# Where the feed-forward weights lie in memory against the activations: 192 bytes off modulo 512 for six products of seven, and one tile for both halves of a weight

## The chip, the core and the metric

The kernel runs on one core of one Trainium2 chip. The metric is the device time of one execution in microseconds (us); before the change it is 2301.29 us, the median of three runs (2299.22, 2301.29 and 2302.05). A core has a matrix engine (PE, TensorE), a vector engine (DVE), a scalar engine (ACT), a small-core engine (POOL) that does next to nothing here, and a queue processor (SP) that issues every DMA of this kernel. Operands of a matmul are read from SBUF, where each of 128 partitions has its own byte addresses; results go to PSUM.

## What is computed

One layer of a hybrid encoder over 512 tokens of width 2048: a normalised input projection, two groups of mixer heads (a gated recurrence called HGRN2, and stick-breaking attention), an output projection with a residual, and then a SwiGLU feed-forward part. The change is about this last part, with a hidden width of 5632 = 44 x 128:

```python
h = rms_norm(x, norm2_g[layer]) * (1.0 + sc2) + sh2
gate, up = jnp.split(h @ w_ffn_in[layer], 2, axis=-1)
x = x + g2 * ((jax.nn.silu(gate) * up) @ w_ffn_out[layer])
```

## The kernel before, in words

**Precision.** TensorE multiplies in the type float32r. To keep float32 accuracy, every operand is split in two halves, a rounded "high" half and the remainder, the "low" half, and each product becomes three matmuls: high x high, high x low, low x high (function `product`, L908; `three`, L227). The function `split` (L212) makes the halves of a weight: ACT casts the raw tile to the high half (L220), DVE subtracts it from the raw tile to give the low half (L221).

**The first feed-forward product** (`h @ w_ffn_in`) is the loop at L1115 over f = 2 to 43, one slice of 128 gate columns and 128 up columns each (f = 0 and 1 are done earlier in another form). Instead of eight block products each f needs seven, by Winograd's scheme: DVE forms sums of weight blocks (L1122 to L1125), and PE runs the products in the order 1, 2, 6, 7, 5, 4, 3. A product is 8 steps of three matmuls, 24 in all, with a stationary weight block of 128x128 and a moving block of activations of 128x256. The activations lie in four tiles, opA (products 1 and 2), opB (6 and 7), opC (5 and 4) and opD (3), and stay there for the whole loop. Between the products ACT copies partial sums out of PSUM ("taps", L1018), DVE adds them up (L1147 to L1150), and for each second f the hidden activations are combined to seven forms, split, and stored to DRAM (`keep`, L1066; tile `forms`).

**Where the weight halves lie.** In the pool `wp` (L137) high and low halves each have a ring of three buffers of 4096 bytes per partition (tags "hi" and "lo", L217 and L218). The whole kernel uses these rings. In the feed-forward loop every fourth call of `split` takes a "spare" pair of tiles instead (`spare_here`, L1105, tags "hi2" and "lo2"). Of the 42 x 7 = 294 products of the loop, 73 have their weights in the spare pair and 221 in the rings. The profile writes the two kinds apart: ff_1h and ff_1l are the halves of product 1 in the rings, ff_1hi and ff_1lo those in the spare pair.

In the built program the rings start at bytes 43808, 47904 and 52000 (high) and 56096, 60192 and 64288 (low) of a partition, which is 288 modulo 512 each time. The activations start at 68384 (opB), 101152 (opC), 133920 (opA) and 166688 (opD), also 288 modulo 512, and one step lies a multiple of 512 behind the other. The spare pair starts at 215008 and 219104, which is 480 modulo 512: 192 bytes further. In all other stages the float32r operands of both sides are at 288 modulo 512.

**What sets the order.** Each engine works through its own list in order. A scheduler in the programming framework arranges these lists when the program is built; `AHEAD` gives splits a higher priority, so that ACT and DVE prepare weights as far ahead of PE as the three rings and the spare pair allow. In the loop each of f = 2 to 17 also takes one row of the conditioning matrix (`ada`, L1060 and L1157: one DMA of 1 MB into a raw buffer and one DVE multiply with sum at L180). Raw weight tiles, gate and up, and these rows share four raw buffers (L171).

**The second feed-forward product** (the loop over `units`) multiplies the stored forms with `w_ffn_out`, seven products by the same scheme, 512 columns wide. At the end the result is transposed with a unit matrix `ident2` (L166, loaded at L306, used at L1220) and stored.

**Small tiles.** `rstd_small` (L237) computes inverse roots for the normalisations of the heads with the small tiles av, y and tmp, two buffers each in the pool of the attention heads.

Of the kernel before, what the change touches and what calls it, by code (L numbers as in the profile page):

```python
# [10 lines left out]
F32 = mybir.dt.float32  # L11
# [118 lines left out]
def trunk(ctx, tc, a):  # L130
# [32 lines left out]
    gain1 = const.tile([P, KT], F32, name="gain1")  # L163
    gain2 = const.tile([P, KT], F32, name="gain2")
    rcol = const.tile([P, 4], F32, name="rcol")
    ident2 = const.tile([P, P], F32, name="ident2")  # L166

    def small_col(base, i=0):
        return small[:, base + i:base + i + 1]
# [37 lines left out]
        nc.sync.dma_start(r, src)  # L207
        return r

    spare, count = [], [0]  # L210

    def split(r, shape, name):  # L212
        count[0] += 1
        if spare and count[0] % 4 == 0:
            hi, lo = spare[0](shape, name)
        else:
            hi = wp.tile(shape, F32R, tag="hi", name=name + "h")  # L217
            lo = wp.tile(shape, F32R, tag="lo", name=name + "l")  # L218
        with tc.high_priority(offset=AHEAD):
            S.copy(hi, r)  # L220
            V.tensor_sub(lo, r, hi.bitcast(F32))  # L221
        return hi, lo
# [12 lines left out]
        V.scalar_tensor_tensor(y, tmp, 1.5, y, op0=ALU.add, op1=ALU.mult)  # L235

    def rstd_small(pool, ss, n, name):  # L237
        av = pool.tile([P, n], F32, tag=f"av{n}", name=f"av{name}")
        y = pool.tile([P, n], F32, tag=f"y{n}", name=f"y{name}")
        tmp = pool.tile([P, n], F32, tag=f"tm{n}", name=f"tm{name}")  # L240
        V.tensor_scalar(av, ss, 1.0 / P, EPS, op0=ALU.mult, op1=ALU.add)
        S.activation(y, av, AF.Ln)
        S.activation(y, y, AF.Exp, scale=-0.5)
        newton(y, av, tmp)
        return y
# [40 lines left out]
    for k in range(KT):  # L286
        xk = xo[:, k]
        if k == 0:
            for i in range(2):
                sl = slice(i * 1024, i * 1024 + 1024)  # L290
                gemv(r0[:, sl], cond[:, sl], lead[:, i:i + 1])
            j = SC1 * KT
            V.scalar_tensor_tensor(mod[:, j:j + 1], lead[:, 0:1], lead[:, 1:2], small_col(C_BADA, j), op0=ALU.add, op1=ALU.add)
            finish_gain(SC1, 0, 1)
            whi = wp.tile([P, 1024], F32R, tag="hi", name="wi0h")
            wlo = wp.tile([P, 1024], F32R, tag="lo", name="wi0l")
            for sl in (slice(0, T), slice(T, 2 * T)):
                S.copy(whi[:, sl], w0[:, sl])
                V.tensor_sub(wlo[:, sl], w0[:, sl], whi[:, sl].bitcast(F32))
        else:  # L300
            nc.sync.dma_start(xk, a["x"][:, k])
            ada(SC1, k)
            if k == 2:
                nc.sync.dma_start(cst, a["cst"])
            if k == KT - 1:
                nc.sync.dma_start(ident2, a["cst"][:, 0])  # L306
            whi, wlo = weights(a["w_hi"][k], [P, 1024], f"wi{k}")
        gk = gain1[:, k:k + 1]
        S.activation(hhi[:, k], xk, AF.Identity, scale=gk)
        V.scalar_tensor_tensor(hlo[:, k], xk, gk, hhi[:, k].bitcast(F32), op0=ALU.mult, op1=ALU.subtract)  # L310
        if k == 0:
            S.activation(ss1, xk, AF.Square)
        else:
            sq = sb.tile([P, T], F32, tag="qT" if k % 2 else "kT", name=f"sq{k}", bufs=1)
            S.activation(sq, xk, AF.Square)
            V.tensor_add(ss1, ss1, sq)
        for n in range(2):
            for t in range(4):
                ts_ = slice(t * P, t * P + P)
                cs = slice(n * T, n * T + T)  # L320
                out = banks[n * 4 + t]
                PE.matmul(out, hhi[:, k, ts_], whi[:, cs], start=(k == 0), stop=False)
                PE.matmul(out, hhi[:, k, ts_], wlo[:, cs], start=False, stop=False)
                PE.matmul(out, hlo[:, k, ts_], whi[:, cs], start=False, stop=(k == KT - 1))
# [684 lines left out]
    def halves_of(r):  # L1009
        return r[:, 0:HALF], r[:, HALF:KT]  # L1010

    def operand(raw, name):
        return split(raw, [P, HALF, P], name)

    def tap(src, name):
# [8 lines left out]
    def place(n):  # L1024
        n %= 11
        return places[0][:, n] if n < 4 else places[1][:, n - 4] if n < 7 else places[2][:, n - 7]
# [76 lines left out]
            later.pop(0)()  # L1103

    def spare_here(shape, name):  # L1105
        return [tp.tile(shape, F32R, tag=t, name=name + t, bufs=1) for t in ("hi2", "lo2")]

    spare.append(spare_here)
    count[0] = 0
# [5 lines left out]
    for f in range(2, FM):  # L1115
        A11, A12 = halves_of(load(a["w_fi"][f, 0], [P, KT, P], f"wg{f}"))
        A21, A22 = halves_of(load(a["w_fi"][f, 1], [P, KT, P], f"wu{f}"))
        S1 = tp.tile([P, HALF, P], F32, tag="sum", name=f"ffS{f}", bufs=3)
        A, B, C = acc(f"ffA{f}")[:, 0:HT], acc(f"ffB{f}")[:, 0:HT], att(f"ffC{f}")[:, 0:HT]
        w1, w2 = operand(A11, f"ff{f}_1"), operand(A12, f"ff{f}_2")  # L1120
        with tc.high_priority(offset=AHEAD):
            V.tensor_add(S1, A21, A22)  # L1122
            V.tensor_sub(A21, A11, A21)
            V.tensor_sub(A11, S1, A11)
            V.tensor_sub(A12, A12, A11)  # L1125
        product(A, w1, 1, True)
        ta = tap(A, f"a{f}")
        one_later()
        product(B, w2, 2, True)
        one_later()  # L1130
        product(A, operand(A11, f"ff{f}_6"), 6)
        tb = tap(A, f"b{f}")
        one_later()
        product(C, operand(A21, f"ff{f}_7"), 7, True)
        t_c = tap(C, f"c{f}")
        one_later()
        product(A, operand(S1, f"ff{f}_5"), 5)
        tu = tap(A, f"u{f}")
        one_later()
        product(C, operand(A22, f"ff{f}_4"), 4)  # L1140
        one_later()
        product(A, operand(A12, f"ff{f}_3"), 3)

        sg = tp.tile([P, T], F32, tag="sg", name=f"sg{f}", bufs=2)
        up = tp.tile([P, T], F32, tag="up", name=f"up{f}", bufs=1)
        with tc.high_priority(offset=2 * AHEAD if f == FM - 1 else 0):
            V.tensor_add(sg[:, 0:HT], B, ta)  # L1147
            S.activation(sg[:, 0:HT], sg[:, 0:HT], AF.Silu)
            V.tensor_add(up[:, HT:T], tu, t_c)
            V.tensor_add(up[:, 0:HT], C, tb)  # L1150
            S.activation(sg[:, HT:T], A, AF.Silu)
        if f == FM - 1:
            begin_second()
        with tc.high_priority(offset=2 * AHEAD if f == FM - 1 else 0):
            keep(f, sg, up)
        if rest:
            rest.pop(0)()  # L1157
# [9 lines left out]
        return [more[:, i * 1024:i * 1024 + n].rearrange("p (k d) -> p k d", k=shape[1]) for i in range(2)]  # L1167

    spare[0] = spare_there


    zp = ctx.enter_context(tc.tile_pool(name="zp", bufs=1, side="right", reuse_waits="tile"))
    T2 = zp.tile([P, 4, T], F32, name="T2")
    zp.tile([P, 512], F32, name="gap")
    O = zp.tile([P, 4, D], F32, name="O")
    A = [att(f"foA{j}") for j in range(2)]
    B = [[acc(f"foB{i}{j}") for j in range(2)] for i in range(2)]
# [52 lines left out]
    for u, (c, i) in enumerate(units):  # L1230
# [8 lines left out]
        if final and i == 0:  # L1239
            for g in range(4):  # L1240
                nc.sync.dma_start(place(7 * c + 7 + g).bitcast(F32).rearrange("p n h t -> p n (h t)"), x1d[:, 4 * g:4 * g + 4])
        y = blocks[u]
        t2 = (T2 if u else yraw[0][:, 2])[:, 0:CHUNKS[c]]
        load_y(u + 1, 2)
# [107 lines left out]
```

## Time and profile before

| what | value |
|---|---|
| median of three runs | 2301.29 us (2299.22 to 2302.05) |
| the profiled execution's own time | 2299.22 us |
| its span in the profile | 2299.2 us |
| granted TensorE clock, mean over the span | 0.994 of full speed |
| busy: ACT | 1160.6 us |
| DMA | 437.69 MB, mean 190 GB/s |
| first feed-forward product, f = 2 to 43 | about 1003.7 to 1849 us of the span |

The span of the profile is the time of that execution, so nothing lies around it; it is 2.1 us under the median. Matmuls are pipelined: a row gives each a modelled duration that runs over the next ones' starts. How fast PE goes is therefore read from the distance between starts.

### The profile page before, as it was taken

The numbers are of one execution on the slowest core, as the hardware profiler recorded it, in microseconds if no ns is written. First come the engines' busy times: TensorE is split into PE (matmuls) and PEld (weight loads), VectorE is DVE, ScalarE is ACT, GpSimd is POOL, SyncE is SP. The second block draws the span as 40 slices with busy tenths as digits, with TensorE's granted clock in tenths as the row PEclk, the third lists the DMA queues.
The fourth block names the chain that finished last, engine by engine and source line by source line (L and its number), as shares of the span: only waits on it lengthen the run. The fifth ranks groups of instructions, "written<-read, shape, count | busy, mean of one in ns | idle before, by whom it ended". The sixth has DMA issues, their size and how long they took to land.

```text
span 2299.2 us, 35729 instructions
## 1 busy us (share of the span) xinstructions
PE 2249.4 (98%) x14171; PEld 2050.2 (89%) x14171; DVE 1917.8 (83%) x2566; ACT 1160.6 (50%) x2015; POOL 10.7 (0%) x25
## 2 busy tenths in 40 slices
PE   7999899999999999999999999999999999999999
PEld 6899899888888788999999999999999977778787
DVE  8887779999888865699899988888888778888888
ACT  4316666565655522564454445454545544544453
POOL 0000000000000000000000000000000000000000
PEclk9999999999999999999999999999999999999999
DMA  9885546853322386346555645454443486665452
GB/s 368 319 317 218 174 145 227 304 183 111 128 93 74 130 303 214 105 151 225 189 204 185 220 143 175 143 174 143 150 160 129 166 314 232 238 220 213 154 200 76
DMA packets 114978, 437.69 MB, mean 190 GB/s; under 512 B 9822, under 2 KB 58236, under 8 KB 76796
## 3 DMA queue, kind: packets, MB, share of 16 engines
q1 hardware_dynamic: 114812, 435.42, 53.0%
q8 instruction: 111, 1.82, 0.3%
q14 instruction: 55, 0.45, 0.1%
HBM read 386.61 MB, written 48.77 MB: 189 GB/s over the span
## 4 chain that ended last, share of the span: by engine, by line
PE 77%; DVE 13%; DMA 3%; issue 3%; ACT 3%; SPq 0%; DVEq 0%; ACTq 0%
PE ffA L93 18%; PE foA L93 9%; PE ffC L93 9%; PE sbp L93 7%; PE wo L93 7%; PE foC L93 4%; PE ffB L93 4%; PE st L93 4%; PE hgf L93 4%; PE hgq L93 3%; PE hgg L93 3%; DMA opd<-fhi 1%; DVE ada L180 1%; DVE yraw L1190 1%; PE l L93 1%
## 5 line engine op out<-in xcount | busy, mean ns | idle before, releaser
L180 DVE SCALAR_TENSOR_TENSOR ada<-ada,cond 128x2048 f32<-128x2048 f32 x95 | 216.8, 2286 | 54.5 <-DMA ada<-in_w_ada 54.3
L93 PE MATMUL ffA<-opD,ff_3h 128*128 128x256 f32 x512 | 93.9, 284 | 1.8 <-ACT u L1018 1.7
L93 PE MATMUL ffA<-opB,ff_6h 128*128 128x256 f32 x512 | 94.1, 284 | 1.0 <-ACT ff_6h L220 1.0
L93 PE MATMUL ffB<-opA,ff_2h 128*128 128x256 f32 x512 | 93.5, 283 | 0.0
L93 PE MATMUL ffC<-opC,ff_4h 128*128 128x256 f32 x512 | 93.5, 283 | 0.0
L93 PE MATMUL ffA<-opC,ff_5h 128*128 128x256 f32 x496 | 90.7, 283 | 0.8 <-ACT b L1018 0.8
L93 PE MATMUL ffA<-opA,ff_1h 128*128 128x256 f32 x496 | 90.6, 283 | 0.0
L93 PE MATMUL ffC<-opB,ff_7h 128*128 128x256 f32 x496 | 90.6, 283 | 0.0
L221 DVE TENSOR_TENSOR wfo_0l<-wfo,wfo_0h 128x1024 fp32r<-128x1024 f32 x48 | 58.7, 1224 | 37.9 <-ACT wfo_0h L220 37.5
L93 PEld LDWEIGHTS ffA<-opD,ff_3h 128*128 128x128 f32 x512 | 79.7, 192 | 2.4 <-ACT u L1018 2.4
L93 PEld LDWEIGHTS ffA<-opB,ff_6h 128*128 128x128 f32 x512 | 80.1, 193 | 1.3 <-ACT ff_6h L220 1.2
L93 PEld LDWEIGHTS ffC<-opC,ff_4h 128*128 128x128 f32 x512 | 79.7, 192 | 0.0
L93 PEld LDWEIGHTS ffB<-opA,ff_2h 128*128 128x128 f32 x512 | 79.7, 192 | 0.0
L220 ACT CAST wfo_0h<-wfo 128x1024 fp32r<-128x1024 f32 x48 | 50.6, 1054 | 57.5 <-PE foA L93 50.4
L1092 ACT CAST fhi<-forms 128x512 fp32r<-128x512 f32 (+1 forms) x63 | 43.6, 692 | 68.5 <-DMA opd<-fhi 59.2
L93 PEld LDWEIGHTS ffA<-opC,ff_5h 128*128 128x128 f32 x496 | 77.2, 192 | 1.0 <-ACT b L1018 1.0
L93 PEld LDWEIGHTS ffC<-opB,ff_7h 128*128 128x128 f32 x496 | 77.3, 192 | 0.0
L93 PEld LDWEIGHTS ffA<-opA,ff_1h 128*128 128x128 f32 x496 | 77.2, 192 | 0.0
L93 PE MATMUL ffA<-opB,ff_6l 128*128 128x256 f32 x256 | 72.7, 284 | 0.0
L93 PE MATMUL ffC<-opC,ff_4l 128*128 128x256 f32 x256 | 72.4, 283 | 0.0
L93 PE MATMUL ffA<-opD,ff_3l 128*128 128x256 f32 x256 | 72.4, 283 | 0.0
L93 PE MATMUL ffB<-opA,ff_2l 128*128 128x256 f32 x256 | 72.4, 283 | 0.0
(1646 smaller groups left out, 7764.6 us busy)
## 6 DMA issues: line engine op xcount, KB each, us to landing
ada<-in_w_ada SPq DMA_DIRECT2D x95, 1024.0 KB, 5.2
wfo<-in_w_fo SPq DMA_DIRECT2D x16, 1024.0 KB, 5.9
yraw<-in_w_fo SPq DMA_DIRECT2D x16, 1024.0 KB, 4.8
fix<-in_w_fix SPq DMA_DIRECT2D x14, 1024.0 KB, 5.6
opd<-forms SPq DMA_DIRECT2D x44, 256.0 KB, 4.3
opd<-fhi SPq DMA_DIRECT2D x42, 256.0 KB, 4.3
opsC<-opd SPq DMA_DIRECT2D x10, 1024.0 KB, 5.1
opsA<-opd SPq DMA_DIRECT2D x9, 1024.0 KB, 7.2
```

Of the source, the lines that this page charges most:

```text
L93: self.engine.matmul(out, lhsT, rhs, **kw)
L180: V.scalar_tensor_tensor(w, w, 1.0, row, op0=ALU.mult, op1=ALU.mult, accum_out=col)
L220: S.copy(hi, r)
L221: V.tensor_sub(lo, r, hi.bitcast(F32))
L1092: S.copy(hi, R[:, q])
L1190: V.tensor_sub(*(t[:, k0:k0 + w] for t in (d, e, g)))
```

## The change

1. `split` takes its two halves from one tile (`ring_pair`): a ring of three tiles of 2176 elements (8704 bytes) per partition, tag "pair", with the high half at element `home` and the low half 1024 elements behind it. 8704 is 17 x 512, so all three tiles have the same place modulo 512.
2. `home` is 0 everywhere but in `operand`, which sets it to 48 elements = 192 bytes for products 1, 2, 6, 7, 5 and 4, and to 0 for product 3 (`aside=False`). After the loop it is 0 again.
3. The spare tiles become 128 elements longer, and their halves begin at element 80 (320 bytes) when `home` is 0, which puts product 3 in the spare pair at 288 modulo 512 too, and at 0 else.
4. Room: av and tmp have one buffer, and `ident2` moves from the constants into what was an unused gap beside the output tile; its DMA moves from the first stage (k = 15) to unit 2 of the second product.

In the built program this gives, in bytes modulo 512:

| product | activations | weights in the rings, before and after | weights in the spare pair, before and after |
|---|---|---|---|
| 1, 2, 6, 7, 5, 4 | 288 | 288, 480 | 480, 480 |
| 3 | 288 | 288, 288 | 480, 288 |

The spare pair is still taken by every fourth split: 73 products of 294, of which 10 are product 3. Everywhere outside the loop the float32r operands stay at 288. `ident2` moves from 96 to 480 modulo 512, where its partner in the transposes lies.

```diff
-    ident2 = const.tile([P, P], F32, name="ident2")
...
-    spare, count = [], [0]
+    spare, count, home = [], [0], [0]
+
+    def ring_pair(shape, name):
+        n = int(np.prod(shape[1:]))
+        t = wp.tile([P, 2048 + 128], F32R, tag="pair", name=name)
+        out = []
+        for b in (home[0], home[0] + 1024):
+            v = t[:, b:b + n]
...
+            out.append(v)
+        return out
...
         if spare and count[0] % 4 == 0:
             hi, lo = spare[0](shape, name)
         else:
-            hi = wp.tile(shape, F32R, tag="hi", name=name + "h")
-            lo = wp.tile(shape, F32R, tag="lo", name=name + "l")
+            hi, lo = ring_pair(shape, name)
...
-        av = pool.tile([P, n], F32, tag=f"av{n}", name=f"av{name}")
+        av = pool.tile([P, n], F32, tag=f"av{n}", name=f"av{name}", bufs=1)
...
-            if k == KT - 1:
-                nc.sync.dma_start(ident2, a["cst"][:, 0])
...
-    def operand(raw, name):
+    def operand(raw, name, aside=True):
+        home[0] = 48 if aside else 0
         return split(raw, [P, HALF, P], name)
...
     def spare_here(shape, name):
-        return [tp.tile(shape, F32R, tag=t, name=name + t, bufs=1) for t in ("hi2", "lo2")]
+        off = 0 if home[0] else 80
+        return [tp.tile([P, 1024 + 128], F32R, tag=t, name=name + t, bufs=1)[:, off:off + 1024]
+                .rearrange("p (a b) -> p a b", a=shape[1]) for t in ("hi2", "lo2")]
...
-        product(A, operand(A12, f"ff{f}_3"), 3)
+        product(A, operand(A12, f"ff{f}_3", False), 3)
...
-    zp.tile([P, 512], F32, name="gap")
+    ident2 = zp.tile([P, 512], F32, name="ident2")[:, 0:P]
...
+        if u == 2:
+            nc.sync.dma_start(ident2, a["cst"][:, 0])
```

Each PE list has the same matmuls as before, and in the feed-forward loop in the same order. Elsewhere the scheduler moves instructions, since it places tiles that are now taken and given back together. Three places:

DVE in the feed-forward loop at f = 12, before: forms10 are the combined activations of f = 10 and 11, ff12_4lo2 is the last low half that reads the raw up weights, and ada91 the row of the conditioning matrix of this f.

```order
L1147 TENSOR_TENSOR sg12_11429<-ffB12_11200,a12_11238 128x256
L1080 TENSOR_TENSOR forms10_10962<-forms10_10962 128x256
L221 TENSOR_TENSOR ff12_4lo2_11374<-wu12r_11196,ff12_4hi2_11373 128x1024
L1081 TENSOR_TENSOR forms10_10962<-forms10_10962 128x256
L1084 TENSOR_TENSOR forms10_10962<-forms10_10962 128x256
L221 TENSOR_TENSOR ff12_3l_11402<-wg12r_11194,ff12_3h_11401 128x1024
L1093 TENSOR_TENSOR forms10_10962<-forms10_10962,fhi11_0_11298 128x768
L221 TENSOR_TENSOR ff13_1l_11450<-wg13r_11441,ff13_1h_11449 128x1024
L180 SCALAR_TENSOR_TENSOR ada91_11665,mod_79<-ada91_11665,cond_72 128x2048
L1124 TENSOR_TENSOR wg13r_11441<-ffS13_11445,wg13r_11441 128x1024
L221 TENSOR_TENSOR ff13_2l_11454<-wg13r_11441,ff13_2h_11453 128x1024
```

The same place after the change:

```order
L1089 TENSOR_TENSOR forms10_10744<-forms10_10744 128x256
L232 TENSOR_TENSOR ff12_4lo2_11147<-wu12r_10973,ff12_4hi2_11146 128x1024
L1090 TENSOR_TENSOR forms10_10744<-forms10_10744 128x256
L1158 TENSOR_TENSOR sg12_11201<-ffB12_10977,a12_11014 128x256
L1093 TENSOR_TENSOR forms10_10744<-forms10_10744 128x256
L232 TENSOR_TENSOR ff12_3_11174<-wg12r_10971,ff12_3_11174 128x1024
L1102 TENSOR_TENSOR forms10_10744<-forms10_10744,fhi11_0_11073 128x768
L232 TENSOR_TENSOR ff13_1_11221<-wg13r_11213,ff13_1_11221 128x1024
L179 SCALAR_TENSOR_TENSOR ada91_11432,mod_79<-ada91_11432,cond_72 128x2048
L232 TENSOR_TENSOR ff13_2_11224<-wg13r_11213,ff13_2_11224 128x1024
L1135 TENSOR_TENSOR wg13r_11213<-ffS13_11217,wg13r_11213 128x1024
```

The sum sg12 now stands between ff12_4lo2 and ada91, and the low half of product 2 of the next f comes one place earlier.

DVE where the last attention head (7) is normalised, before: whq0 are weights of the first HGRN2 head, rows7 the head's queries and keys.

```order
L233 SCALAR_TENSOR_TENSOR tmsb7_3773<-avsb7_3771,ysb7_3772 128x8
L221 TENSOR_TENSOR whq0_8l_3937<-whq0r_3903,whq0_8h_3936 128x1024
L234 TENSOR_TENSOR tmsb7_3773<-tmsb7_3773,ysb7_3772 128x8
L180 SCALAR_TENSOR_TENSOR ada67_4017,mod_79<-ada67_4017,cond_72 128x2048
L235 SCALAR_TENSOR_TENSOR ysb7_3772<-tmsb7_3773,ysb7_3772 128x8
L180 SCALAR_TENSOR_TENSOR ada72_4042,mod_79<-ada72_4042,cond_72 128x2048
L401 TENSOR_TENSOR rows7_3737<-rows7_3737,ysb7_3772 128x4x256
```

The same place after the change:

```order
L244 SCALAR_TENSOR_TENSOR tmsb7_3690<-avsb7_3688,ysb7_3689 128x8
L245 TENSOR_TENSOR tmsb7_3690<-tmsb7_3690,ysb7_3689 128x8
L246 SCALAR_TENSOR_TENSOR ysb7_3689<-tmsb7_3690,ysb7_3689 128x8
L232 TENSOR_TENSOR whq0_8_3851<-whq0r_3819,whq0_8_3851 128x1024
L409 TENSOR_TENSOR rows7_3655<-rows7_3655,ysb7_3689 128x4x256
L179 SCALAR_TENSOR_TENSOR ada67_3931,mod_79<-ada67_3931,cond_72 128x2048
L179 SCALAR_TENSOR_TENSOR ada72_3956,mod_79<-ada72_3956,cond_72 128x2048
```

rows7 now stands ahead of the two rows ada67 and ada72 instead of behind them.

PE at the transposes of rows7 (qkt7), before: they stand 11 matmuls into the second projection (hgq0) of the first HGRN2 head.

```order
L93 MATMUL hgq0_3902<-hhi_84,whq0_0l_3906 128x512
L93 MATMUL hgq0_3902<-hhi_84,whq0_0h_3905 128x512
L93 MATMUL hgq0_3902<-hlo_85,whq0_0h_3905 128x512
L98 MATMUL qkt7_3818<-cst_90,rows7_3737 128x128 x8
L93 MATMUL hgq0_3902<-hhi_84,whq0_0l_3906 128x512
```

After, they stand ahead of the last 8 matmuls of the first projection (hgf0), and the head's next products (zA7, zB7) follow before these are through:

```order
L98 MATMUL qkt7_3734<-cst_89,rows7_3655 128x128 x8
L93 MATMUL hgf0_3669<-hlo_84,whf0_8_3728 128x512
L93 MATMUL hgf0_3669<-hhi_83,whf0_8_3728 128x512 x2
L93 MATMUL hgf0_3669<-hlo_84,whf0_8_3728 128x512
L93 MATMUL hgf0_3669<-hhi_83,whf0_8_3728 128x512 x2
L93 MATMUL zA7_3768<-kT7_3744,qT7_3743 128x128
L93 MATMUL zA7_3768<-kT7_3744,qT7_3743 128x384
L93 MATMUL zB7_3781<-kT7_3744,qT7_3743 128x256
```

The transposes stand 19 projection matmuls earlier on PE, and what follows of this head and of the first three HGRN2 heads is interleaved with the projections in another way.

More of the change, by code (lines that the diff above doesn't have):

```diff
@@ L208, in load @@
         return r
-    spare, count = [], [0]
+    spare, count, home = [], [0], [0]
[5 more added lines that the diff above has]
+            v = t[:, b:b + n]
+            if len(shape) == 3:
+                v = v.rearrange("p (a b) -> p a b", a=shape[1])
+            elif len(shape) == 4:
+                v = v.rearrange("p (a b c) -> p a b c", a=shape[1], b=shape[2])
+            out.append(v)
+        return out
     def split(r, shape, name):
@@ L237, in rstd_small @@
     def rstd_small(pool, ss, n, name):
-        av = pool.tile([P, n], F32, tag=f"av{n}", name=f"av{name}")
+        av = pool.tile([P, n], F32, tag=f"av{n}", name=f"av{name}", bufs=1)
         y = pool.tile([P, n], F32, tag=f"y{n}", name=f"y{name}")
-        tmp = pool.tile([P, n], F32, tag=f"tm{n}", name=f"tm{name}")
+        tmp = pool.tile([P, n], F32, tag=f"tm{n}", name=f"tm{name}", bufs=1)
         V.tensor_scalar(av, ss, 1.0 / P, EPS, op0=ALU.mult, op1=ALU.add)
@@ L294, in trunk @@
             finish_gain(SC1, 0, 1)
-            whi = wp.tile([P, 1024], F32R, tag="hi", name="wi0h")
-            wlo = wp.tile([P, 1024], F32R, tag="lo", name="wi0l")
+            whi, wlo = ring_pair([P, 1024], "wi0")
             for sl in (slice(0, T), slice(T, 2 * T)):
@@ L1169, in trunk @@
     spare[0] = spare_there
+    home[0] = 0
     zp = ctx.enter_context(tc.tile_pool(name="zp", bufs=1, side="right", reuse_waits="tile"))
     T2 = zp.tile([P, 4, T], F32, name="T2")
-    zp.tile([P, 512], F32, name="gap")
+    ident2 = zp.tile([P, 512], F32, name="ident2")[:, 0:P]
     O = zp.tile([P, 4, D], F32, name="O")
```

## The prediction, made before the changed kernel ran

> **What bounds the kernel now.** The page first: who is busy, and what the chain that ended last consists of.
>
> ```profile
> PE 2249.4 (98%) x14171; PEld 2050.2 (89%) x14171; DVE 1917.8 (83%) x2566; ACT 1160.6 (50%) x2015; POOL 10.7 (0%) x25
> PE 77%; DVE 13%; DMA 3%; issue 3%; ACT 3%; SPq 0%; DVEq 0%; ACTq 0%
> ```
>
> PE carries the end. So I ask stage by stage how closely its matmuls follow each other, and who would keep it waiting if they followed faster. The stages of the first feed-forward product, cut where an f begins (us, then PE, weight loads, DVE and ACT busy, granted clock, DMA):
>
> ```profile
> 1003.68:1090.69 87.01, 82.14 (x674) 81.33 (x673) 82.84 (x97) 41.05 (x61) 0.00 (x0) 0.98 0.59 206
> 1172.30:1292.26 119.96, 119.90 (x1010) 119.68 (x1009) 110.22 (x123) 59.13 (x87) 0.00 (x0) 1.00 0.57 204
> 1392.15:1630.71 238.56, 238.56 (x2019) 238.56 (x2017) 197.02 (x223) 120.20 (x174) 0.00 (x0) 1.00 0.44 153
> ```
>
> With 168 matmuls to an f, the second row is 6 of them (f = 10 to 15), the third 12 (f = 21 to 32). Late in the loop an f takes 238.56/12 = 19.88 us, PE is never idle, and DVE works 197.02/12 = 16.42 us of it. In the middle DVE works 110.22/6 = 18.37 us per f, and PE takes 119.96/6 = 19.99.
>
> Now the timeline of PE over two neighbouring products at f = 27, the first with weights in the spare pair, the second in the rings (start in us, us from start to modelled end; a row of x2 is two matmuls):
>
> ```profile
> 1511.39 0.28 PE L93 MATMUL ffA<-opD,ff_3l 128*128 128x256 f32 x1
> 1511.51 0.39 PE L93 MATMUL ffA<-opA,ff_1hi 128*128 128x256 f32 x2
> 1511.74 0.28 PE L93 MATMUL ffA<-opA,ff_1lo 128*128 128x256 f32 x1
> ...
> 1514.23 0.40 PE L93 MATMUL ffB<-opA,ff_2h 128*128 128x256 f32 x2
> 1514.47 0.28 PE L93 MATMUL ffB<-opA,ff_2l 128*128 128x256 f32 x1
> ...
> 1517.11 0.40 PE L93 MATMUL ffA<-opB,ff_6h 128*128 128x256 f32 x2
> ```
>
> The 24 matmuls from the spare pair take 1514.23 - 1511.51 = 2.72 us, 113.3 ns each; the 24 from the rings 1517.11 - 1514.23 = 2.88 us, 120.0 ns each, with the same shape and the same activations (opA), at a granted clock of 1.00. Modelled durations show that this is no accident of one f (groups over the loop: busy us, mean ns):
>
> ```profile
> L93 PE MATMUL ffA<-opD,ff_3h 128*128 128x256 f32 x505 | 92.7, 284 | 1.8 <-ACT u L1018 1.7
> L93 PE MATMUL ffA<-opA,ff_1h 128*128 128x256 f32 x496 | 90.6, 283 | 0.0
> L93 PE MATMUL ffA<-opA,ff_1hi 128*128 128x256 f32 x176 | 30.5, 276 | 0.0
> L93 PE MATMUL ffA<-opD,ff_3hi 128*128 128x256 f32 x160 | 27.8, 276 | 0.0
> ```
>
> 284 and 283 ns from the rings, 276 from the spare pair, for opA as for opD. Rings and activations lie on the same place modulo 512, the spare pair 192 bytes behind it. The change puts six products of seven of the rings where the spare pair is.
>
> **The change part by part.** *Six products aside.* Before, 221 products run at 2.88 us and 73 at 2.72. After, the 42 of product 3 run at 2.88 and 252 at 2.72. So 221 - 42 = 179 products become 0.16 us shorter: 28.6 us, or 28.6/42 = 0.68 us per f, if nothing but PE bounds the loop. The 10 of product 3 that leave the spare pair's place are in this count. An f then needs 6 x 2.72 + 2.88 = 19.20 us of PE.
>
> The row says that the place of the weights costs 6.7 ns a matmul. The Trainium skill (TensorE: Matmul & The Clock Gate, section Step-by-step: what each phase is for) says otherwise: the array has two independent SBUF read ports, and loading the next weights takes no read bandwidth from the running matmul. By the rows the sum is 28.6 us, by that rule it is nothing; the trace speaks against the rule, with 113.3 against 120.0 ns for one shape, unless something else sets the spare pair apart.
>
> *Who keeps up.* f = 2 to 17 each take a row of the conditioning matrix. First f = 2, PE's waits from 1003.68 to 1031.17, then all of them from there to 1332.47 (us in total, times, longest):
>
> ```profile
> PE ffC L93 <- ACT ff_7hi L220: 2.3, 1, 2.3
> PE ffA L93 <- ACT ff_6h L220: 1.0, 1, 1.0
> PE ffA L93 <- ACT b L1018: 0.8, 1, 0.8
> PE ffA L93 <- DVE ff_1l L221: 0.8, 1, 0.8
> ...
> PE ffA L93 <- ACT u L1018: 1.7, 2, 1.5
> ```
>
> f = 2 waits for weights four times, so shorter matmuls there only wait longer: I take 0 of its 0.68. For f = 3 to 17 the question is DVE's own pace, from its waits in the middle stage (six f):
>
> ```profile
> DVE ada L180 <- DMA ada<-in_w_ada: 6.6, 6, 1.4
> DVE forms L1093 <- ACT fhi L1092: 1.1, 3, 0.4
> DVE ff_7l L221 <- ACT ff_7h L220: 0.8, 3, 0.3
> DVE ffS L1122 <- DMA wu16r<-in_w_fi: 0.3, 1, 0.3
> DVE ff_1lo L221 <- ACT ff_1hi L220: 0.3, 1, 0.3
> DVE ff_1l L221 <- ACT ff_1h L220: 0.2, 1, 0.2
> ```
>
> DVE waits for the DMA of each conditioning row, 6.6/6 = 1.10 us: that load (L176) is held in SP's queue until ff_4's low half or the forms behind it are done, as SP's waits in the same stage show:
>
> ```profile
> SPq L176 <- DVE forms L1081: 36.2, 3, 12.1
> SPq L176 <- DVE ff_4l L221: 20.3, 3, 6.9
> ```
>
> This doesn't shrink with PE. With 0.05 for the up weights DVE needs 18.37 + 1.10 + 0.05 = 19.52 us per f, and 2.4/6 = 0.40 more if its waits for ACT stay too: 19.92. PE wants 19.20. So DVE sets the pace here. The scheduler's move helps a little: the sum sg12, now between ff12_4lo2 and ada91, fills some of that wait, in every second f:
>
> ```profile
> 1300.21 0.41 DVE L1147 TENSOR_TENSOR sg<-ffB,a 128x256 f32<-128x256 f32 x1
> 1307.03 2.29 DVE L180 SCALAR_TENSOR_TENSOR ada<-ada,cond 128x2048 f32<-128x2048 f32 x1 [0.97 <-DMA ada<-in_w_ada]
> ```
>
> 0.41 of the 0.97 us, 0.2 per f. Between 19.3 and 19.9 I take 19.5, near the sum without the waits for ACT, since the rings' waits end when PE takes weights faster: 15 x (19.9 - 19.5) = 6.0 us. The bounds are 0 (DVE holds 19.99) and 15 x 0.68 = 10.2 (the lead that DVE has built up covers the difference).
>
> f = 18 to 43 have no such row; DVE's 16.42 us fit into 19.20 (86%), and PE doesn't wait there at all in the row above (238.56 busy of 238.56). 26 x 0.68 = 17.7 us, whole.
>
> *One tile for both halves.* The high half's buffer comes back with the last matmul of its product instead of the last but one, 0.12 us later. ACT meets this in its casts, which run up to three products ahead of PE: nothing on the path; without that cover 0.12 us per product.
>
> *What the scheduler moves in the mixers.* PE reaches the transposes of rows7 19 matmuls earlier, and DVE has rows7 ready earlier by the two conditioning rows now behind it. Before:
>
> ```profile
> 447.89 2.28 DVE L180 SCALAR_TENSOR_TENSOR ada<-ada,cond 128x2048 f32<-128x2048 f32 x1
> ...
> 450.18 2.29 DVE L180 SCALAR_TENSOR_TENSOR ada<-ada,cond 128x2048 f32<-128x2048 f32 x1
> ...
> 452.39 1.22 DVE L401 TENSOR_TENSOR rows<-rows,ysb 128x1024 f32<-128x1024 f32 x1
> ```
>
> That is 452.39 - 447.89 = 4.5 us; PE's 19 matmuls, by starts of this stage, are shorter than that or equal:
>
> ```profile
> 577.07 0.39 PE L93 MATMUL hgf<-hhi,whf_8h 128*128 128x512 f32 x1
> 577.30 0.39 PE L93 MATMUL hgf<-hlo,whf_8h 128*128 128x512 f32 x1
> ```
>
> 19 x 0.23 = 4.4 us. The two cancel. PE's waits around this, from 430 to 560 and from 540 to 1000, bound what can be won:
>
> ```profile
> PE tA L98 <- ACT I L446: 0.9, 1, 0.9
> PE qkt L98 <- DVE rows L401: 0.5, 1, 0.5
> ...
> PE wo L93 <- DVE olo L801: 1.6, 1, 1.6
> PE wo L93 <- ACT ohi L800: 1.3, 1, 1.3
> ```
>
> I take 0, with 3 us to either side: a gain of these waits (3 of their 4.3 us), or new ones like them.
>
> *Small things.* One buffer for av and tmp, written again a head later: nothing, or one DVE wait. The DMA of ident2 leaves the queue ahead of the first stage's last weights and enters it in unit 2 of the second product, ahead of a load for the next unit, and is needed only at the end: an issue time of 0.3 to 0.4 us either way. The 64 transposes with ident2 now read both sides at 480: at most the 6.7 ns that place costs in the loop, 0.4 us. All within the 3 us.
>
> **The sum.** 0 + 6.0 + 17.7 = 23.7 us. Against the profiled execution, 2299.2 - 23.7 = 2275.5; the median before stands 2.1 higher, so about 2277 for the median.
>
> **The rivals.** *DVE holds f = 3 to 17 entirely* at 19.99 us, and only the 17.7 of the late f are won: 2301.3 - 17.7 = 2283.6. For it: 18.37 + 1.10 + 0.45 = 19.92 is within 0.1 of what an f takes there now. Against: PE hardly waits there today (1.7 us), so DVE has some lead.
>
> *The place in SBUF, not the offset.* The spare pair is the only weight tile near the top of the partition (byte 215008; the rings start at 43808). If that makes it fast, the rings stay at 120.0 ns and the time is 2301. Against: the gain is the same for opA to opD, which lie 98000 bytes apart. The rule of independent ports that the Trainium skill states (TensorE: Matmul & The Clock Gate, the section above) would give this time too.
>
> *Slower: off the activations costs more in the rings.* No row shows a ring product at 192 bytes. Were it 6.7 ns slower instead of faster, 252 - 63 = 189 ring products would lose 0.16 us each and the 10 of product 3 that leave the fast place as well: 199 x 0.16 = 31.8 us, 2333. It decides from 120.0 ns per ring matmul on. Against: 73 products at this very offset are all fast.
>
> **How the numbers follow.** The forecast 0.82, DVE holding 0.09, the place 0.06, slower 0.03. The first two are faster; of the place 0.05 is no change, 0.01 slower through the mixers. A measurement tells about 0.2% (4.6 us) from no change. So faster 0.91, same 0.05, slower 0.04. The range: the best is 28.6 + 3 = 31.6, f = 2 gaining too, 2269.7; the worst 17.7 - 3 = 14.7, 2286.6. It holds the first two cases.
>
> **What would show it.** Timeline of the late loop: 2.72 us for products 1, 2, 6, 7, 5 and 4 whichever tile holds the weights, 2.88 for product 3 always, 19.2 us for an f. Middle stage: 19.3 to 19.6 us per f, DVE at 94% or more, and PE waits for weights or taps that it hadn't before. f = 2 as long as now, 27.5 us (1031.17 - 1003.68). Equal times before 1000 and after the loop. Wrong if a ring product off the activations still takes 2.88 us, if the middle stage shrinks as much as the late one (DVE no bound) or not at all, or if the mixers move by over 3 us.

## The result: ten to eleven microseconds instead of twenty-four, and the profile after

| | before | after |
|---|---|---|
| median of six runs each, us | 2302.91 (2299.22 to 2306.12) | 2292.14 (2288.73 to 2296.81) |
| ratio, 95% interval | | 0.9956 [0.9944, 0.9969] |
| profiled span, us | 2299.2 | 2286.7 |

The change is faster by 10.8 us between the medians, by 10.1 us by the ratio. Forecast were 2277, with a range up to 2286.6, so it gained less than half and the measured time lies outside the range. One thing in the sections above has to be put right: the span of a profile is not the whole time of its execution. After the change, and in all runs below, the time lies 1.7 to 2.2 us above the span (2288.73 against 2286.7 for the profiled one), and in the runs of the kernel before beside them 2.1 to 2.2. The profile before with its span of 2299.2 is therefore most likely that of the run of 2301.29, not that of 2299.22. The forecast for the median doesn't change with that.

First the page of the changed kernel, busy engines and the chain that ended last.

```profile
PE 2228.2 (97%) x14171; PEld 2025.8 (89%) x14171; DVE 1915.4 (84%) x2566; ACT 1156.0 (51%) x2015; POOL 10.0 (0%) x25
PE 64%; DVE 20%; DMA 7%; issue 5%; ACT 3%; SPq 0%; DVEq 0%; ACTq 0%
```

PE is busy for 21.2 us less, but the span is only 12.5 us shorter, and PE's share of the chain has fallen from 77% to 64%. DVE and DMA now carry 27% of it, 16% before. Something other than PE ends last in places. Where, the starts of product 1 in the timelines of PE tell; cut there, the two profiled executions are (us):

| | before | after | forecast gain | gain |
|---|---|---|---|---|
| start of f = 2 | 1003.68 | 1003.12 | 0 | 0.6 |
| f = 2 | 27.50 | 26.18 | 0 | 1.3 |
| f = 3 to 17 | 301.30 | 300.15 | 6.0 | 1.15 |
| f = 18 to 43 | 516.96 | 507.39 | 17.7 | 9.6 |
| from the loop's end to the span's | 449.8 | 449.9 | 0 | -0.1 |

All that is missing is missing in the loop. PE's matmuls there do what was forecast. The timeline after, f = 25, a row of x24 is a whole product from the rings (start in us):

```profile
1466.84 2.88 PE L93 MATMUL ffA<-opA,ff 128*128 128x256 f32 x24
1469.56 2.88 PE L93 MATMUL ffB<-opA,ff 128*128 128x256 f32 x24
...
1475.00 2.88 PE L93 MATMUL ffC<-opB,ff 128*128 128x256 f32 x24
1477.72 2.88 PE L93 MATMUL ffA<-opC,ff 128*128 128x256 f32 x24
```

From start to start 2.72 us per ring product, 113.3 ns a matmul. Of the 25 late f, f = 18 to 42, 18 take the 19.20 us that were forecast. The other seven don't. The stages again (us, then PE, weight loads, DVE and ACT busy, granted clock, DMA), f = 10 to 15 and f = 21 to 32, and PE's waits from f = 3 to the end of the loop (us in total, times, longest):

```profile
1170.24:1289.23 118.99, 117.26 (x1011) 116.60 (x1009) 107.81 (x122) 57.84 (x87) 0.00 (x0) 1.00 0.55 200
1389.08:1622.52 233.44, 231.95 (x2019) 231.55 (x2018) 196.49 (x223) 118.24 (x175) 0.00 (x0) 1.00 0.45 156
```

```profile
PE ffC L93 <- ACT c L1027: 6.1, 7, 1.6
PE ffA L93 <- ACT u L1027: 4.0, 3, 2.1
PE ffA L93 <- ACT a L1027: 0.8, 1, 0.8
PE ffA L93 <- ACT b L1027: 0.7, 1, 0.7
```

The late stage has PE idle for 1.49 us of twelve f, where before it was never idle. PE waits 11.6 us for taps, the copies that ACT makes of a partial sum before PE may write into that bank again. Why a tap is late shows the chain of waits around f = 34 (start, length, what):

```profile
1634.05 7.64 DMA wu35r<-in_w_fi
1641.71 0.04 DVE ffS L1133
...
1649.45 1.22 DVE ff L232
1650.67 0.35 DVE forms L1093
1651.04 0.84 ACT fhi L1101
1651.88 0.03 ACT sg L1159
1651.90 3.31 DMA opd<-fhi
...
1655.29 0.04 ACT fhi L1101
1655.33 0.48 issue
1655.81 1.04 ACT ff_1hi L231
1656.85 0.28 ACT c L1027
1657.13 0.04 issue
1657.17 3.10 PE ffC L93 x24
```

It begins with the load of the up weights of f = 35, which took 7.64 us here and 4.9 us in the kernel before; no run shows why. DVE has the sum ffS of that f early in its list and waits there for the load, with the forms behind it. The forms come late, so ACT's cast of them (fhi) does; the next cast needs the same buffer, whose store must land first; and behind that cast, in ACT's list, stands tap c of f = 34. DVE's waits for up weights are new in this size; from f = 3 on, the five longest of eighteen:

```profile
DVE ffS L1133 <- DMA wu35r<-in_w_fi: 2.8, 1, 2.8
DVE ffS L1133 <- DMA wu8r<-in_w_fi: 2.5, 1, 2.5
DVE ffS L1133 <- DMA wu31r<-in_w_fi: 2.3, 1, 2.3
DVE ffS L1133 <- DMA wu19r<-in_w_fi: 2.1, 1, 2.1
DVE ffS L1133 <- DMA wu43r<-in_w_fi: 2.1, 1, 2.1
```

All eighteen make 25.2 us, against seven with 3.1 before. The long ones in the late stage are for wu19, 23, 31, 35 and 43, and the f in front of them, 18, 22, 30, 34 and 42, are five of the seven late f that take over 19.20 us.

Against an ideal f of 6 x 2.72 + 2.88 = 19.20 us, the distances from start to start of all matmuls split the lost time so (us; a wait counts with the late start of the second matmul behind it, and "restarts" are single late matmuls without a wait in the profile):

| | f = 3 to 17, before | after | f = 18 to 42, before | after |
|---|---|---|---|---|
| PE waits | 2.6 | 8.3 | 0.0 | 6.5 |
| half clock, restarts | 0.4 | 1.9 | 0.0 | 0.3 |
| spacing above 113.3 (product 3: 120.0) | 10.3 | 1.9 | 17.1 | 1.4 |

The last row holds a second surprise: after some waits products off the activations go at 118 ns instead of 113.3. And DVE's share of f = 10 to 15 is 91% (107.81 of 118.99 us), where the prediction named 94% or more as the sign of DVE's pace.

### The profile page after: what moved, and what is told of

Same layout as the page of the kernel before. It is cut to its first block, busy times and chain, and to the rows that moved or that the text cites. A ratio compares the mean times of both kernels' runs of the same rounds, so it can differ in the third digit from the quotient of the medians.

```text
span 2286.7 us, 35537 instructions
## 1 busy us (share of the span) xinstructions
PE 2228.2 (97%) x14171; PEld 2025.8 (89%) x14171; DVE 1915.4 (84%) x2566; ACT 1156.0 (51%) x2015; POOL 10.0 (0%) x25
## 4 chain that ended last, share of the span: by engine, by line
PE 64%; DVE 20%; DMA 7%; issue 5%; ACT 3%; SPq 0%; DVEq 0%; ACTq 0%
PE ffA L93 10%; PE foA L93 9%; PE wo L93 7%; PE sbp L93 7%; PE ffC L93 5%; PE foC L93 4%; PE st L93 4%; PE hgf L93 3%; PE hgg L93 3%; PE hgq L93 3%; DVE ff L232 3%; DMA opd<-fhi 2%; PE ffB L93 2%; PE ff L93 2%; DVE ada L179 1%
## 5 line engine op out<-in xcount | busy, mean ns | idle before, releaser
L93 PE MATMUL sbp<-wsb,hhi 128*128 128x384 f32 x1024 | 269.8, 343 | 3.1 <-DVE wsb L232 1.7
L93 PEld LDWEIGHTS sbp<-wsb,hhi 128*128 128x128 f32 x1024 | 185.2, 190 | 7.9 <-issue 3.3
L93 PE MATMUL sbp<-wsb,hlo 128*128 128x384 f32 x512 | 172.9, 338 | 0.0
L93 PE MATMUL wo<-ohi,wo 128*128 128x512 f32 x480 | 150.2, 392 | 4.1 <-ACT wo L231 1.6
L93 PE MATMUL ffA<-opD,ff 128*128 128x256 f32 x768 | 99.0, 286 | 4.0 <-ACT u L1027 4.0
L93 PE MATMUL ffC<-opC,ff 128*128 128x256 f32 x768 | 94.7, 279 | 5.8 <-ACT c L1027 5.8
L93 PEld LDWEIGHTS ffA<-opD,ff 128*128 128x128 f32 x768 | 95.6, 194 | 4.5 <-ACT u L1027 4.5
L93 PEld LDWEIGHTS sbp<-wsb,hlo 128*128 128x128 f32 x512 | 97.0, 190 | 0.8 <-issue 0.5
L93 PE MATMUL ffA<-opB,ff 128*128 128x256 f32 x768 | 93.3, 277 | 1.7 <-ACT ff L231 1.0
L93 PE MATMUL wo<-olo,wo 128*128 128x512 f32 x240 | 93.5, 390 | 0.1
```

What stands on the lines that cost most here:

```text
L93: self.engine.matmul(out, lhsT, rhs, **kw)
```

## The experiments

All are edits of the changed kernel; ratios are against the kernel before, run beside it. The stage times come from the starts of product 1 in each profiled execution.

**E1, a second buffer for the casts.** The first suspect was the last link of the chain, the single buffer fhi.

```diff
-                hi = tp.tile([P, b - a, HT], F32R, tag="fhi", name=f"fhi{f}_{a}", bufs=1)
+                hi = tp.tile([P, b - a, HT], F32R, tag="fhj" if a == 3 else "fhi", name=f"fhi{f}_{a}", bufs=1)
```

> Theory (ACT's queue stands still on the one buffer for the high halves of the hidden activations, whose store must land, and the taps behind it come too late for PE): the stalls of the late f (f = 18 to 42, 488.2 us instead of 25 x 19.2 = 480.0) nearly go: 480 to 483.5 us, the time 5 to 8 us below the changed kernel's 2292, so 2284 to 2287. In the waits of ACT the row of the cast of the hidden activations on its store's DMA (76.2 us, 35 times) falls under 20 us. Rival (weights come late, because their loads stand behind the stores of the hidden activations in SP's queue, and those wait for DVE): f = 18 to 42 stay at 486 to 490 us and the time at 2290 to 2293, though ACT's row goes. Both: f = 3 to 17 stay between 19.8 and 20.05 us each.

Measured: 2292.08 us (2286.17 to 2295.19), 0.9954 [0.9941, 0.9966]; f = 18 to 42 took 489.0 us, f = 3 to 17 302.2 (20.15 each, a little above the 20.05 expected). The wait of the cast on its store halved to 38.0 us, the time didn't move. The first theory falls: DVE's waits for up weights stayed (28.4 us), and what ACT no longer waited for its store it waited for DVE's forms (37.8 us, 28.1 in the changed kernel).

**E2, the one tile alone,** with every weight where it lay before the change: in `operand` `home[0] = 0`, in `spare_here` `off = 0`.

> Keeps the one tile for both halves and all of the order, and puts the weights back where they lay before: rings on the activations, spare pair 192 bytes off. Theory (the order itself costs nothing; the stalls need the shorter products): as the kernel before, 2303 plus or minus 2.5 us, f = 18 to 42 at 497 plus or minus 1, hardly a wait of PE for taps. Rival (the one tile and the order that the scheduler makes of it bring the stalls): 2307 to 2312 us, and the stalls of 0.6 to 1.9 us at f = 18, 22, 30, 34 stand here too.

Measured: 2301.02 us, 0.9996 [0.9987, 1.0004]; f = 18 to 42 497.7 us, f = 3 to 17 300.5. One row tells the late stage, twelve f without any idle time of PE:

```profile
1390.84:1629.40 238.56, 238.56 (x2019) 238.56 (x2017) 198.72 (x224) 120.08 (x174) 0.00 (x0) 1.00 0.45 155
```

The new order of the lists, with the same DVE work, costs and gains nothing while PE takes 19.88 us per f. The stalls need the shorter products.

**E3, all products on the activations:** as E2, but the spare pair keeps `off = 80`.

> All products, in the spare pair too, have their weights on the activations modulo 512 bytes. Theory (the offset alone sets 120.0 or 113.3 ns): 120.0 ns for all matmuls of the loop, an f takes 20.16 us late, 73 x 0.16 = 11.7 us more than with the spare pair off: 2313 to 2317 us. Rival (the spare pair is fast because of where it lies in the partition): 113 ns stay in the spare pair, and 2303 us.

Measured: 2308.9 us, 1.0029 [1.0018, 1.0040]. All products went at 120.0 ns, the spare pair's too, and an f of the late stage at 20.16 us (241.92 us for twelve):

```profile
1396.05:1637.97 241.92, 241.92 (x2019) 241.92 (x2018) 198.24 (x223) 119.76 (x174) 0.00 (x0) 1.00 0.45 152
```

So the offset and not the place near the top of the partition made the spare pair fast. The loop was 11.2 us longer than in E2's profile, as expected, but the medians lie only 7.9 apart, and the time missed its interval by 4 us. In part that is the choice of executions: the profiles are of E3's slowest (2311.44) and of one of E2's fastest (2299.86). The rest stays open.

**E4, no conditioning rows in the loop:** the line `rest += ...` is replaced by a constant, which leaves out the 16 rows of the last gate with their DMAs and DVE sums.

> Leaves out the 16 conditioning rows of the last gate, with their DMAs and DVE sums; a constant stands in their place. Theory (DVE and the rows set the pace of f = 3 to 17, 20.01 us each): those f fall to 19.3 to 19.5 us, 8 to 11 us less in all, f = 2 by 0 to 2 more, and the time is 2279 to 2284. Rival (the taps' lateness sets the pace there as in the late f, with or without rows): 19.6 us and more, 2286 us and above. The late f keep their stalls in both (487 to 489 us).

Measured: 2284.69 us, 0.9927 [0.9914, 0.9939]; f = 3 to 17 293.8 us (19.6 each), f = 18 to 42 491.6. Without an eighth of DVE's work in the middle stage (2.29 of 18.37 us per f) an f still took 19.6 instead of 19.2. The rows cost 6 us, but DVE's sum of work is not what sets the pace. The stage agrees with the rival, the time lies between the two expected intervals, and the late f, expected at 487 to 489 us, took 3.4 us more than in the changed kernel: DVE's waits for up weights grew to 35.3 us.

**E5, one sum buffer.** With `bufs=1` instead of 3 for the tile ffS its sum has to wait for the low half of product 5, and comes behind the forms in DVE's list.

> One buffer instead of three for the sum ffS of the up weights, nothing else: DVE then gets that sum of the next f only behind the low half of product 5 of this f, some nine instructions later than now, and no longer stands in its queue waiting for the up weights' DMA with the forms, low halves and sums of this f behind it. Theory (DVE's wait for late up weights, 25.2 us in the loop against 3.1 before the change, is what makes the forms, ACT's casts of them and so the taps late): that wait falls under 6 us, PE's waits for taps under 4 us, f = 18 to 42 take 480 to 483.5 us instead of 488.2, the time is 2282 to 2287. Rival (ACT's own queue, or the store of the hidden activations, is late by itself): f = 18 to 42 stay at 486 to 490 us, the time at 2289 to 2294. For f = 3 to 17 the theory expects 19.4 to 19.9 us each.

Measured: 2290.85 us, 0.9951 [0.9938, 0.9963]. The late stage did what the theory said, twelve f at 19.20 us with PE never idle, and 480.0 us for f = 18 to 42; DVE's wait for up weights was 0.6 us in the whole loop.

```profile
1390.78:1621.18 230.40, 230.40 (x2018) 230.40 (x2017) 198.13 (x223) 120.26 (x174) 0.00 (x0) 1.00 0.45 159
```

The time didn't follow. In f = 3 to 17 (305.5 us, 20.4 each, expected 19.4 to 19.9) 5.4 us went: PE waited there 9.7 us for taps, and the granted clock was twice at 0.50 for 3.4 us. Behind the loop 7.2 us went, 6.4 of them where the first copy into O waits for the last store of the forms (PE, then ACT):

```profile
PE foA L93 <- ACT O L1217: 10.1, 1, 10.1
```

```profile
ACT O L1217 <- DMA opd<-forms: 6.3, 1, 6.3
```

In the changed kernel that wait of PE is 3.7 us. So the time missed its interval too. A total that stands still can hide a stage that was won whole.

**E6, a fifth raw buffer** in the room that E5 frees, on top of E5's edit; the loop's loads of gate and up weights go through `load5`:

```diff
+    def load5(src, name):
+        nth[0] += 1
+        if nth[0] % 5:
+            return load(src, [P, KT, P], name)
+        r = tp.tile([P, KT, P], F32, tag="raw5", name=name + "r", bufs=1)
+        nc.sync.dma_start(r, src)
+        return r
```

> As the one with a single sum buffer, and of the gate and up loads of the loop every fifth goes to a buffer of its own, so that loads start earlier. Theory (the loads are late because a raw buffer comes free late): DVE's waits for weights and conditioning rows fall below those of the single sum buffer alone, and f = 3 to 17 shrink by 2 to 6 us more: 2278 to 2284. Rival (the place of the sum is all there is to it): the same time as with the single sum buffer alone, within 2 us.

Measured: 2274.39 us, 0.9879 [0.9864, 0.9894]; f = 3 to 17 294.2 us, f = 18 to 42 480.0, behind the loop 450.4. The time is below both expected intervals. PE's waits from f = 3 on are 3.9 us instead of 11.6:

```profile
PE ffC L93 <- ACT c L1037: 3.1, 3, 1.7
PE ffA L93 <- ACT b L1037: 0.6, 1, 0.6
PE ffA L93 <- ACT a L1037: 0.2, 1, 0.2
```

f = 11 to 14 take 19.20 us each here, with their conditioning rows.

**E7, off in every stage:** `home` is 48 throughout, product 3 included.

> All float32r weights of the rings lie 192 bytes off the activations modulo 512, product 3 and the other stages too (projections, mixers, second feed-forward product; there every fourth product stays on the activations). Theory (the 6.7 ns per matmul are a matter of the place alone, whatever the shape, with the weights stationary or moving): matmuls of 512 columns follow each other at 220 ns instead of 226.7, and where PE sets the pace it counts: some 4000 to 5000 matmuls, 25 to 32 us less than the changed kernel, 2258 to 2268. Rival (in those stages loads or DVE set the pace, or it works only with 256 columns): 2280 to 2292.

Measured: 2307.63 us, 1.0024 [1.0013, 1.0035], 15 us slower than the changed kernel. Neither theory had this. In the first stage six matmuls of 512 columns take 65.57 - 64.17 = 1.40 us, 233 ns each:

```profile
64.17 1.56 PE L93 MATMUL st<-wi,hhi 128*128 128x512 f32 x6
65.57 0.63 PE L93 MATMUL st<-wi,hlo 128*128 128x512 f32 x2
```

In the changed kernel, on the activations, six take 64.46 - 63.10 = 1.36 us, 226.7 each:

```profile
63.10 1.52 PE L93 MATMUL st<-wi,hhi 128*128 128x512 f32 x6
64.46 0.84 PE L93 MATMUL st<-wi,hlo 128*128 128x512 f32 x3
```

With 512 columns, where the weights are the moving side, 192 bytes off is slower. Where they are stationary (the output projection, tile wo) it gains nothing either: mostly 226 to 232 ns against 226 to 227. And in the loop nearly all products, at the very addresses at which they go at 113.3 ns in the changed kernel, went at 118: an f of 19.79 us. In the profiles the loop takes 11.1 us more than in the changed kernel, and the stages ahead of it and behind it 5.4 each.

**E8, distances.** Each f of the loop has another `home`, from 0 to 124 elements, the spare pair 192 bytes more.

> In each f of the loop another distance between weights and activations, from 0 to 496 bytes in the rings, 192 bytes more in the spare pair. Theory (only the same place modulo 512, or one within a few tens of bytes of it, costs): 120.0 ns at 0, 113.3 ns from 64 to 448 bytes. Rival (it is a matter of one particular distance): 113.3 ns near 192 only, other distances at 116 to 120 ns.

Measured: 2306.66 us, a single execution. Neither theory holds. At 192 bytes, f = 33, the rings gave 118, not 113.3:

```profile
1635.60 2.99 PE L93 MATMUL ffA<-opA,ff 128*128 128x256 f32 x24
1638.43 2.99 PE L93 MATMUL ffB<-opA,ff 128*128 128x256 f32 x24
```

(2.83 us.) At 256 bytes, f = 14, they gave 120.0, as on the activations:

```profile
1254.28 3.04 PE L93 MATMUL ffA<-opA,ff 128*128 128x256 f32 x24
1257.16 3.04 PE L93 MATMUL ffB<-opA,ff 128*128 128x256 f32 x24
```

(2.88 us.) The spare pair did the same wherever it came to lie 256 or 512 bytes off (f = 8, 16, 29, 37). Two f whose distances differ by 256 go alike, product by product, but for the choice between 113.3 and 118: at 160 bytes (f = 32) as at 416 (f = 40) the means of the seven products lie at the same values from 118.7 to 120.2 ns. And 113.3 ns stands only at 64, 320 and 448 bytes, where the rings also gave 118. So in this one execution the place counts modulo 256 rather than 512, and only odd multiples of 64 bytes reach 113.3 ns, and not always. With E7 it led to another question: what E7 and E8 lack is product 3 on the activations.

**E9, only product 3 off as well:** `home[0] = 48` in `operand`, the other stages as they are.

> The changed kernel with product 3 off the activations too, the other stages as they are. Theory (off the activations the matmuls have two steady spacings, 113.3 and 118 ns; a wait of PE throws them into the slow one, and only matmuls on the activations, product 3, bring the fast one back): after the waits of f = 2 nearly all products of the loop go at 118 ns, a late f takes 168 x 0.118 = 19.8 us instead of 19.2, and the time is 2297 to 2303, slower than the changed kernel by 5 to 10. Rival (the place alone sets the spacing, and 118 ns is chance): 113.3 ns for product 3 as well, 19.04 us per undisturbed f, 42 x 0.16 = 6.7 us less than the changed kernel: 2284 to 2288.

Measured: 2298.32 us, 0.9983 [0.9974, 0.9992]; f = 18 to 42 496.6 us, PE never idle in f = 21 to 32:

```profile
1392.56:1630.00 237.44, 237.44 (x2019) 237.44 (x2017) 197.86 (x223) 120.42 (x174) 0.00 (x0) 1.00 0.45 155
```

```profile
1502.80 2.99 PE L93 MATMUL ffA<-opC,ff 128*128 128x256 f32 x24
1505.62 2.99 PE L93 MATMUL ffC<-opC,ff 128*128 128x256 f32 x24
1508.45 2.99 PE L93 MATMUL ffA<-opD,ff 128*128 128x256 f32 x24
```

2.83 us for every product, 6 us more in all than with product 3 on the activations. The theory stands in the main: off the activations there are two steady spacings, and a product on them mostly brings the fast one back (in the changed kernel after 12 of the 14 f whose product 4 went at 118). Its word "only" doesn't stand. In f = 16 of this run, after a wait of 1.2 us, product 3 went at 113.3 ns, and f = 17 took 19.04 us, all seven products off; in f = 18 it was over.

**E10, E6's buffers with the weights where they lay before** (E2's two edits on E6).

> The fifth raw buffer and the single sum buffer, with the weights where they lay before the change (rings on the activations, spare pair off). Theory (late weights cost only where PE is faster; before the change the slack of 1.3 us covered them): f = 18 to 42 stay at 497 to 498 us, f = 3 to 17 go from 301 to 298 to 300, the time is 2298 to 2302, and so what the change is worth with this buffer is 24 to 28 us, its full sum. Rival (the fifth buffer gains by itself, whatever the place): 2284 to 2290.

Measured: 2299.17 us, 0.9991 [0.9983, 1.0000]; f = 18 to 42 497.1 us, f = 3 to 17 299.7. The buffers alone gain almost nothing, and with them the place gains 2299.2 - 2274.4 = 25 us.

**E11, one sum buffer and two cast buffers** (E1 and E5 together).

> One sum buffer, and the room it frees given to a second buffer for the high halves of the hidden activations instead of a fifth raw buffer. Theory (f = 3 to 17 are short of raw buffers: each of them loads three tiles into four buffers): f = 3 to 17 stay at 300 to 306 us, the time at 2284 to 2292. Rival (any relief of ACT's queue does what the fifth raw buffer did): f = 3 to 17 at 293 to 296 us, the time at 2273 to 2278. Both: f = 18 to 42 at 480 to 481 us.

Measured: 2279.02 us, 0.9906 [0.9891, 0.9922]; f = 3 to 17 292.7 us, f = 18 to 42 480.0, and the wait of 10.1 us behind the loop that E5 has. That is near the rival, at most 1 us outside its intervals. So the middle stage was not short of raw buffers in particular, as I had said: a second cast buffer does as much once the sum is out of the way.

**E12, all three.**

> All three of the earlier edits on the changed kernel: one sum buffer, a fifth raw buffer, a second buffer for the high halves of the hidden activations. If the fifth raw buffer and the second cast buffer relieve different waits of f = 3 to 17, these fall from 294.2 and 292.7 to about 290 us and the time is 2269 to 2273; if both relieve the same chain, 292 to 294 us and 2272 to 2275. Both: f = 18 to 42 at 480.0 us, and no wait of 10 us at the start of the second product, since that wait was there only in the two kernels without a fifth raw buffer.

Measured: 2274.48 us, 0.9881 [0.9866, 0.9896]; f = 3 to 17 293.4 us, f = 18 to 42 480.0. Of the middle stage, f = 12 to 17 took 19.20 us each, with their conditioning rows:

```profile
1209.70:1324.90 115.20, 115.20 (x1010) 115.20 (x1009) 108.37 (x122) 60.18 (x87) 0.00 (x0) 1.00 0.57 204
```

DVE works 94% of that (18.06 us per f), waits 0.2 us for the rows in all six f, and PE is never idle. The two buffers relieve the same chain. E6, and E12 within its spread, beat both kernels of this case, by 28 us before and by 18 after the change.

## Why the prediction was wrong

**Right:** the spacing of 113.3 ns at 192 bytes off, in the rings as in the spare pair, for all four activation tiles, and 120.0 for product 3; equal times before f = 2 and after the loop; that the place in the partition doesn't matter (E3). The Trainium skill (TensorE: Matmul & The Clock Gate, section Step-by-step: what each phase is for) has weight loads take no read bandwidth from the running matmul; 120.0 ns in E3 against 113.3, with nothing changed but the offset, speak against it here. f = 2 was forecast to stay at 27.5 us and took 26.2, but so it did in E2 (26.4), with the weights where they lay before: the place didn't do that.

**The step that failed first:** "f = 18 to 43 ... 26 x 0.68 = 17.7 us, whole". It came out as 9.6. The reason given was that DVE's 16.42 us fit into 19.20 and that PE never waited there. Both were true and neither was the question. DVE was busy for 84% (196.49 of 233.44 us), but its list is in order: the sum ffS stands ahead of the forms and waits for a load, and a tap stands at the end of that chain. PE had not waited because tap c came just before it was needed. At f = 34 of the kernel before, ACT and PE:

```profile
1663.15 0.36 ACT L1018 COPY c<-ffC 128x256 f32<-128x256 f32 x1
```

```profile
1664.79 0.40 PE L93 MATMUL ffC<-opC,ff_4h 128*128 128x256 f32 x2
```

The tap ended at 1663.15 + 0.36 = 1663.51, PE took its bank at 1664.79: 1.3 us of slack, under 7% of an f, and 1.3 to 1.5 us in every late f of that kernel. Nothing in that chain got shorter with PE's products, so the shorter f ate from this slack: the forms are made once in two f, which together became 2 x 0.64 = 1.28 us shorter. In the changed kernel PE took the bank 0.05 us behind the tap's end, with no slack left, in f = 18, 22, 30, 34 and 42. E5 shows that this chain was the cause by taking the sum out of the forms' way: 480.0 us. Of the 8.2 us lost in f = 18 to 42, 6.5 were waits, 0.3 restarts and 1.4 the slow spacing.

**The second:** "so DVE sets the pace here", 6.0 us in f = 3 to 17, measured 1.15. There is no such pace: in E12 six f with all their DVE work run at 19.20 us, and in E4, with 2.29 us less per f, they take 19.6. The sum of 19.52 us was the wrong measure. In the changed kernel's f = 10 to 15 it came out smaller: 107.81/6 = 17.97 of work, 0.92 of waiting for the rows and 1.6/6 = 0.27 for up weights, 19.16 us, under PE's 19.20, and yet an f took 118.99/6 = 19.83. The rest of DVE's time went in waits for ACT. The row for the conditioning rows:

```profile
DVE ada L179 <- DMA ada<-in_w_ada: 5.5, 6, 1.7
```

(5.5/6 = 0.92. The 6.0 us also counts from 19.9 us per f, where the row before had 19.99; from there it would have been 7.4, farther off still.) Here too it is the chain of waits, which takes 5.7 us more than before, with 1.5 more at half clock and 1.9 in the slow spacing against 10.3 from the shorter products. What still holds these f at 19.5 to 19.6 in E6, E11 and E12 stays open.

**Not seen at all** was the second spacing, though the kernel before has it: products 5 of f = 7 and 6 and 3 of f = 13 came from the spare pair at 118 ns, so the 73 products at that offset were not all fast, as the prediction has it. The full sum of 28.6 us was a fair size for the place itself: E10 to E6 is 25. The rivals missed as well. "DVE holds f = 3 to 17" had that stage's size right, next to nothing won, but not its cause, and with the late f won whole its 2283.6 missed as well. The slower case was priced for the rings of the loop, where 192 bytes off cost at most 118 ns, while E7 shows it for 512 columns.

## What to carry to other kernels

Before a faster engine is credited with its full gain, look at the last link that it waits for, not at the busy shares: how many microseconds before its use does a tap, a weight or a buffer come, and what in that chain stands in order behind a DMA? A gain of 3% per period is eaten from a slack of 6%, as here, once that chain jitters by a few microseconds; the place of one instruction in a list or one buffer more can bring it back. And compare stage by stage: E5's equal total held a stage won whole and two lost ones.

## What the runs showed of the hardware

**Two spacings off the activations.** In the changed kernel the second matmul of product 4 of f = 26 comes 74 ns late (187 instead of 113 ns after the first). The profile shows no wait there, but tap c had ended only 0.09 us ahead of the product. From there on the products off the activations go at 118 ns, through f = 27, with nobody waiting:

```profile
1508.25 2.99 PE L93 MATMUL ffB<-opA,ff 128*128 128x256 f32 x24
1511.08 1.10 PE L93 MATMUL ffA<-opB,ff 128*128 128x256 f32 x8
```

(2.83 us.) During product 3 of f = 26 the distances were 121, 120, 124, 117, 118 and so on; during product 3 of f = 27 they settled at 120 each, and f = 28 went at 113 again. Not every wait does it: after one of 0.6 us in f = 8 the next product went on at 113. What holds the stream in one spacing or the other, no run shows.

**A short wait can cost the clock.** At f = 8 PE waited for 2.37 us (from start to start, as the lengths below), and the clock granted then was 0.50 for 3.3 us (stages: us, PE, weight loads, DVE, ACT and POOL busy, clock, DMA):

```profile
1143.56:1145.90 2.34, 0.27 (x3) 0.07 (x1) 2.30 (x2) 0.91 (x3) 0.00 (x0) 1.00 1.10 401
...
1146.70:1150.00 3.30, 3.30 (x17) 3.30 (x17) 3.14 (x4) 0.82 (x2) 0.00 (x0) 0.50 1.01 400
1150.00:1153.00 3.00, 3.00 (x28) 3.00 (x28) 2.44 (x3) 2.20 (x4) 0.00 (x0) 1.00 0.59 219
```

17 matmuls in 3.30 us instead of 28, some 1.5 us on top of the wait. After 1.85 us at f = 34 it stayed at 1.00:

```profile
1657.20:1660.50 3.30, 3.30 (x28) 3.30 (x29) 3.27 (x4) 1.14 (x2) 0.00 (x0) 1.00 1.01 362
```

The Trainium skill (TensorE: Matmul & The Clock Gate, section Why this matters for your kernels) advises against idle gaps of PE above about 3 us; here 2.37 sufficed. The length alone doesn't decide: a wait of 2.03 us in E1 was followed by 0.50, one of 2.04 us in E7 and one of 2.21 us in E10 were not.
